# Hybrid decoder layer: conditioning parts 2 and 3 in whole, evenly spaced visits from a ring of four tiles of their own; part 4 from the shared ring in the output stage

## The chip, the cores and the metric

One core of a Trainium2 chip runs the kernel. The metric is device time in microseconds (us) of one execution. Three runs of the kernel before give a median of 1353.53 us, lowest 1352.69, highest 1353.59.

## The reference, cut to what matters

One layer of a hybrid decoder on 288 columns of tokens (256 of a prompt and 8 short sequences of 4), width 2048. Cut to what the kernel's stages and the change need:

```python
mod = silu(c) @ w_ada + b_ada                  # 9 conditions, 6 parts of 2048: "ada"
sh1, sc1, g1, sh2, sc2, g2 = split(mod, 6)     # parts 0, 1, 2, 3, 4, 5
h = rmsnorm(x, norm1) * (1 + sc1) + sh1
u_pool, z, xbc, dt = split(h @ w_in)           # one projection
pool_out = pool_mixer(u_pool)                  # trailing windows 2, 4, 8, 16, a linear map per group
ssd_out = rmsnorm(ssd(conv(xbc), dt) * silu(z))# 24 heads, 4 groups
x = x + g1 * (concat(pool_out, ssd_out) @ w_out)
h2 = rmsnorm(x, norm2) * (1 + sc2) + sh2
x = x + g2 * conv_ffn(h2)                      # gate, val and down projections
```

Part 2 (`g1`) is wanted first where the output projection is added to `x`; parts 3 and 4 (`sh2`, `sc2`) first where `h2` is made, ahead of the feed-forward stage.

## The kernel before, in words

**Stages.** The stages follow one another on the tensor engine (PE): the `xbc` projection in blocks of output tiles, then `mm_uz_*` (z and pooling columns), then the output projection `mm_out_0` to `mm_out_15`, then up/gate/val and down. Each projection multiplies a 128x128 weight block with 128x288 operands in three passes (lines 303, 304, 305: `whi*h`, `whi*l`, `wlo*h`), in a rounded 32-bit format. ACT casts each raw tile of weights to `whi` (L289) and DVE makes the rest `wlo` (L291).

**Work between.** While PE runs these projections, generators of other work are pulled a step at a time, and a scheduler orders each engine's instructions by priority and program order. `back` is the scan: its PE work (`cse`, `y`, `xt`, `bt`, `cb`, `s`, `yo`) is in plain 32-bit, a matmul of it being issued as several records. `late` is the pooling mixer: DVE makes `pout`, PE multiplies it (`pool`, L888). `adas` is the conditioning.

**Conditioning parts 2, 3, 4.** `ada_part_units` streams 32 tiles a part (`raw_adap`, 512 KB each: row block k, half h). `ada_mm` (L332) multiplies each tile twice into four 32-column strips of one accumulator `adap`, in plain 32-bit: a matmul is two records, so a tile is 4 records. A visit, the step between two yields, is `AY = 2` row blocks: 4 tiles, 8 matmuls, 16 records. When a part's eight visits are done, ACT copies the sum out (`asb_p`, L337), PE transposes it into an auxiliary accumulator (`adat_p`, L343), and DVE adds the bias in four instructions (`ada<-adat_p`, L420). The accumulator tiles called `aux` are shared by `adat_p`, `cse`, `y`, `pool` and others. Between `mm_dt` (the end of what both kernels have alike) and the feed-forward stage there are 24 visits.

**What sets their order.** `pull(adas, RA1 / AY)` in the last `xbc` block, `pull(adas, RA2 / AY)` in the uz stage and a pull after each `mm_out_m` add credit; at 1 a step is taken. The eight matmuls of a visit have no tie to one another: the scheduler may put other ready work between them.

**Tiles and queue.** All raw tiles, those of the projections and of the conditioning, come from one ring: 16 slots (`RAW0` 8 in pool `w0` and `RAW1` 8 in pool `w1`) up to the last `xbc` block, where `w0` is dropped, then 8, and 9 from `mm_out_5`. Every load is issued by SP, in program order, and a load waits on SP until its slot's last reader is done.

Of the kernel before, what the change touches and what calls it, by code (L numbers as in the profile page):

```python
# [25 lines left out]
NC9 = 1 + NB  # L26
# [10 lines left out]
ET = XT + len(UEARLY) + 3 * ZEARLY  # L37
EPS = 1e-6
WU = (14, 2, 2, 2, 6)
RAW0, RAW1, RAW2 = 8, 8, 1  # L40
SPLIT0, SPLIT1, SPLIT2 = 1, 2, 2
YK = 2
AQ = (4, 4, 4, 4, 4, 4)
# [5 lines left out]
TP = 0.4  # L49
TV, TL = 2.0, 2.8  # L50
GB = 4
AY = 2

RA1, RA2, RB1, RB2, RB3 = 0.5, 0.4, 1.0, 1.0, 1.0
TA, ADA_OUT = 4, 4
TK = 4
GA = (2, 3)
XM = (0, 2, 5, 9)
# [106 lines left out]
def kernel(ctx: ExitStack, tc, ins, outs):  # L165
# [98 lines left out]

    wp = [None]

    def load(key):
        off, cols = S.items[key]
        t = wp[0].tile([P, RAWC], F32, tag="raw", name="raw_" + "_".join(map(str, key)))
        nc.sync.dma_start(t[:, :cols], wflat[off:off + P * cols].rearrange("(p n) -> p n", p=P))  # L270
        return t

# [3 lines left out]

    def top_up():

        while queue and nloads[0] - min((n for n, _ in ahead.values()), default=nloads[0]) < RAW0 + RAW1:
            key = queue.popleft()  # L280
            ahead[key] = (nloads[0], load(key))
            nloads[0] += 1
# [69 lines left out]
    def ada_group_units(gi):  # L352
# [49 lines left out]
            nc.vector.tensor_tensor(o, src, b.unsqueeze(3).to_broadcast([P, 2, nj // 2, NC9]), ALU.add)  # L402
        ada_scale(0, 1, early[:, V_N1:V_N1 + KT], k0, gk)

    def ada_part_units(part, ay=1):
        ps = pa.tile([P, 512], F32, tag="ada", name=f"adap{part}")
        for k in range(KT):
            raws = [load(("adap", part, k, h)) for h in range(2)]
            for h in range(2):
                ada_mm(ps, raws[h], k, 0, 512, range(2 * h, 2 * h + 2))  # L410
            if k % ay == ay - 1:
                yield
        asb = ada_sb(ps, 512, f"p{part}")
        yield
        pt = ada_tr(asb, 512, f"p{part}")
        for i in range(4):
            o = ada[:, part].rearrange("p (j i) c -> p j i c", j=4)[:, :, i, :]
            b = bada[:, part].rearrange("p (j i) -> p j i", j=4)[:, :, i]
            src = pt[:, i * P:(i + 1) * P].rearrange("p (j c) -> p j c", j=4)[:, :, 0:NC9]
            nc.vector.tensor_tensor(o, src, b.unsqueeze(2).to_broadcast([P, 4, NC9]), ALU.add)  # L420
        if part == 4:
            ada_scale(1, 4, vec[:, V_N2:V_N2 + KT], 0, KT)
        yield

    def samp(ap):
        return ap.rearrange("p (b l) -> p b l", b=NB)
# [30 lines left out]
    class _W:  # L457


        def __init__(self):  # L460
            self.slots = {"raw": [], "whi": [], "wlo": []}
            self.i = {"raw": 0, "whi": 0, "wlo": 0}

        def add(self, pool, nraw, nsp):
            for tag, n in (("raw", nraw), ("whi", nsp), ("wlo", nsp)):
                m = len(self.slots[tag])
                if m:
                    r = self.i[tag] % m
                    self.slots[tag] = self.slots[tag][r:] + self.slots[tag][:r]
                    self.i[tag] = 0  # L470
                self.slots[tag] += [(pool, n)] * n

        def drop(self, pool):
            for tag, sl in self.slots.items():
                r = self.i[tag] % len(sl)
                self.slots[tag] = [x for x in sl[r:] + sl[:r] if x[0] is not pool]
                self.i[tag] = 0

        def tile(self, shape, dt, tag, name):
            pool, n = self.slots[tag][self.i[tag] % len(self.slots[tag])]  # L480
            self.i[tag] += 1
            return pool.tile(shape, dt, tag=tag, name=name, bufs=n)

    wp[0] = _W()
    wp[0].add(ctx.enter_context(tc.tile_pool(name="w1", bufs=1, side="right")), RAW1, SPLIT1)
    mx_ctx = ExitStack()
    mx = mx_ctx.enter_context(tc.tile_pool(name="mx", bufs=1))
    xa = []
# [10 lines left out]
    w0_ctx = ExitStack()  # L499
    w0 = w0_ctx.enter_context(tc.tile_pool(name="w0", bufs=1))  # L500
    shift(w0, 32)
    wp[0].add(w0, RAW0, SPLIT0)
    sx = [None]

    cvp = [mx.tile([P, 5, CW], F32, tag="cvp", name=f"cvp{g}", bufs=4) for g in range(4)]
# [159 lines left out]
    def drain(gen):  # L665
        for _ in gen:
            pass
# [236 lines left out]
    def chain(*gens):  # L904
        for gn in gens:
            yield from gn

    adas = chain(*(ada_part_units(p, AY) for p in (2, 3, 4)))
# [78 lines left out]
    def pull(gn, rate):  # L987

        credit[id(gn)] = credit.get(id(gn), 0.0) + rate
        while credit[id(gn)] >= 1:  # L990
            credit[id(gn)] -= 1
            next(gn, None)

    nloads[0] = len(first) + KT // 4
    for bi in range(len(BLOCKS)):
        last = bi + 1 == len(BLOCKS)
        top_up()
        if last:

            wp[0].drop(w0)  # L1000
            w0_ctx.close()
            sx[0] = mx_ctx.enter_context(tc.tile_pool(name="sx", bufs=1, reuse_waits="tile"))
            raw = load(("dt",))[:, :KT * NH].rearrange("p (k h) -> p k h", h=NH)
            wdt = wp[0].tile([P, RAWC], F32R, tag="whi", name="whi_dt")
            with tc.high_priority():
                nc.gpsimd.memset(wdt.bitcast(F32), 0.0)
                both = wdt[:, :DTW * KT].rearrange("p (k c) -> p k c", c=DTW)
                nc.scalar.copy(both[:, :, 0:NH], raw)
                nc.vector.tensor_tensor(both[:, :, 32:32 + NH], raw, both[:, :, 0:NH].bitcast(F32), ALU.subtract)
            ps = pm.tile([P, 512], F32, tag="mm", name="mm_dt")  # L1010
# [4 lines left out]
            late_states()  # L1015
            dt_stage(ps)
        elif bi == 4:
            nc.sync.dma_start(vec, ins["vec"])
        elif bi == 5:
            late_loads()  # L1020
        for i, m in enumerate(xbc_units(bi)):
            if not last:
                top_up()
                if bi == 0 and i in (3, 7, 13):
                    ci = {3: 2, 7: 3, 13: 4}[i]
                    ready["xbc", 0, ci] = split(fetch(("xbc", 0, ci)), 0, len(_xbc_chunks(0)[ci][1]) * P,
                                                f"xbc0_{ci}", pin=True)
                if i in VIS[bi]:
                    next(nxt)
                    top_up()  # L1030
            else:
                pull(back, 0.5 if m < 20 else RB1) if m >= 9 else None
                pull(adas, RA1 / AY)

    late = {}
    n = 0
# [1 line left out]
    for m in list(range(4 + 3 * ZEARLY, 16)) + ULATE:  # L1038
        for _ in uz_units(m):
            n += 1  # L1040
            for gn in late.values():
                pull(gn, 0.5)
            pull(adas, RA2 / AY)
            pull(back, RB2 if n <= zlast else RB3)
            if n == zlast:
                drain(back)
                back = ssd3
        if m < 4:
            late[m] = pool_units(m)
            next(late[m])  # L1050
    pull(adas, TA / AY)
    for h, (_, n) in enumerate(_halves(KT)):
        ready[("out", 0, h)] = split(load(("out", 0, h)), 0, n * P, f"out_0_{h}")
    drain(back)
# [33 lines left out]
    for i in range(KT // YK):  # L1088
        ps0 = next(out0)
        if i == 1:  # L1090
            for gn in late.values():
                drain(gn)
            for g in MIXK[NZ:]:
                mix_pool(g)
        if i == 3:
            psq = aux("ysum")
            col_sums(psq, ssq, ones[:, 0:1], True, True)
            _, rstdy = rstd_of(psq, NH * 64, "rstdy")
    mx_ctx.close()
    ff = ctx.enter_context(tc.tile_pool(name="ff", bufs=1, reuse_waits="tile"))  # L1100
    w2 = ctx.enter_context(tc.tile_pool(name="w2", bufs=1, reuse_waits="tile"))
# [49 lines left out]
    for m in range(16):  # L1151
        if m in XM:
            sl = slice(4 * XM.index(m), 4 * XM.index(m) + 4)
            nc.sync.dma_start(x[:, sl, :], ins["x"][:, sl, :])
        if m == 5:
            wp[0].add(w2, RAW2, SPLIT2)
        if m == 0:
            out_norm(ps0[0], m)
        else:
            for i, (pz, pp) in enumerate(out_units(m)):  # L1160
                if m == KT - 1 and i == 5:
                    all_but_last("ssum2")
# [295 lines left out]
```

## Time and profile before

| what | value |
|---|---|
| time, median of 3 runs | 1353.53 us |
| profiled execution: its time, its span | 1353.11 us, 1351.3 us |
| instructions | 26246 |
| PE busy | 1337.3 us (99%), 10517 matmul records |
| weight loads (PEld) | 1247.5 us (92%) |
| DVE, ACT, POOL busy | 820.0 us (61%), 579.4 us (43%), 227.5 us (17%) |
| moved by DMA | 323.19 MB |
| granted clock | 0.998 |

Times inside the trace are from the start of the span. In a line of the timeline the columns are start, length (from the first start of the run of alike instructions to the last end), engine, line, operation, output and inputs, shapes and count, and in brackets the idle time before it and what ended it. Matmuls overlap: a 128x288 pass is shown as 290 ns long, and the next starts 130 ns later. Idle of PE is the gap that its records leave; it is 14.0 us in the whole span (1351.3 less 1337.3).

### The profile page before, as it was taken

The page shows a single profiled execution, that of the slowest core. Times are in us where ns is not written, and L with a number is a line of the kernel's source. Part 1 is how long each engine was busy: PE and PEld are TensorE (multiplying, and loading weights), DVE is VectorE, ACT ScalarE, POOL GpSimd, SP SyncE. Part 2 cuts the span into 40 slices and gives each one's busy share as a digit, 9 for nine tenths or more (in the row PEclk, how much of TensorE's full clock was granted, in tenths as well). Part 3 has the DMA queues.
Part 4 walks back from the last instruction along what each step waited for, and adds up shares of the span by engine and source line. Part 5 has one row for each costly group of instructions (what it writes and reads, how often), then busy time and mean ns, then how long its engine had stood idle before and what let it go on. Part 6 is the DMA issues. An engine that isn't in the chain of part 4 may idle for free.

```text
span 1351.3 us, 26246 instructions
## 1 busy us (share of the span) xinstructions
PE 1337.3 (99%) x10517; PEld 1247.5 (92%) x10517; DVE 820.0 (61%) x1394; ACT 579.4 (43%) x911; POOL 227.5 (17%) x449
## 2 busy tenths in 40 slices
PE   9999999999999999999999999999999999999997
PEld 8889997776789889999999999999999999999997
DVE  5776568778665568645665445656655556566543
ACT  5343244587733335434443333434433343444442
POOL 0000012122122223111211001321120011132221
PEclk9999999999999999999999999999999999999999
DMA  9999768978888877787555555655555565566531
GB/s 373 405 408 368 252 242 324 340 257 295 324 332 323 320 253 257 249 280 265 181 187 182 162 178 183 204 183 196 181 180 164 184 191 184 187 207 194 179 119 70
DMA packets 97482, 323.19 MB, mean 239 GB/s; under 512 B 10768, under 2 KB 19920, under 8 KB 97360
## 3 DMA queue, kind: packets, MB, share of 16 engines
q1 hardware_dynamic: 93600, 310.79, 66.3%
q0 software_dynamic: 3184, 9.69, 2.0%
q8 instruction: 82, 1.34, 0.4%
q10 hardware_dynamic: 576, 1.03, 0.2%
q14 instruction: 40, 0.33, 0.1%
HBM read 309.78 MB, written 10.39 MB: 237 GB/s over the span
## 4 chain that ended last, share of the span: by engine, by line
PE 74%; DVE 1%; issue 0%; ACT 0%; DVEq 0%
PE mm_down L304 7%; PE mm_down L303 7%; PE mm_down L305 7%; PE mm_gate L303 6%; PE mm_val L304 6%; PE mm_gate L304 6%; PE mm_val L305 6%; PE mm_gate L305 6%; PE mm_val L303 6%; PE adap L332 3%; PE mm_out L303 2%; PE mm_out L304 2%; PE mm_out L305 2%; PE mm_up L303 1%; PE mm_up L304 1%; PE mm_up L305 1%
## 5 line engine op out<-in xcount | busy, mean ns | idle before, releaser
L304 PE MATMUL mm_down<-al,whi_down 128*128 128x288 f32 x688 | 202.5, 294 | 0.0
L303 PE MATMUL mm_down<-ah,whi_down 128*128 128x288 f32 x688 | 202.4, 294 | 0.0
L305 PE MATMUL mm_down<-ah,wlo_down 128*128 128x288 f32 x688 | 202.0, 294 | 0.0
L304 PE MATMUL mm_val<-h2l,whi_val 128*128 128x288 f32 x640 | 189.1, 296 | 0.0
L304 PE MATMUL mm_gate<-h2l,whi_gate 128*128 128x288 f32 x640 | 189.1, 295 | 0.0
L303 PE MATMUL mm_gate<-h2h,whi_gate 128*128 128x288 f32 x640 | 188.8, 295 | 0.0
L305 PE MATMUL mm_val<-h2h,wlo_val 128*128 128x288 f32 x640 | 188.4, 294 | 0.0
L305 PE MATMUL mm_gate<-h2h,wlo_gate 128*128 128x288 f32 x640 | 188.4, 294 | 0.0
L303 PE MATMUL mm_val<-h2h,whi_val 128*128 128x288 f32 x640 | 187.9, 294 | 0.0
L291 DVE TENSOR_TENSOR wlo_gate<-raw_gate,whi_gate 128x1024 fp32r<-128x1024 f32 x80 | 98.4, 1230 | 136.4 <-ACT whi_gate L289 136.3
L291 DVE TENSOR_TENSOR wlo_down<-raw_down,whi_down 128x1024 fp32r<-128x1024 f32 x96 | 107.5, 1120 | 116.9 <-ACT whi_down L289 114.4
L289 ACT CAST whi_down<-raw_down 128x1024 fp32r<-128x1024 f32 x96 | 92.3, 961 | 167.0 <-PE mm_down L304 118.0
L289 ACT CAST whi_gate<-raw_gate 128x1024 fp32r<-128x1024 f32 x80 | 83.8, 1049 | 160.0 <-PE mm_gate L304 64.9
L289 ACT CAST whi_val<-raw_val 128x1024 fp32r<-128x1024 f32 x80 | 84.1, 1051 | 119.5 <-issue 101.9
L303 PE MATMUL xbc<-h1h,whi_xbc 128*128 128x288 f32 x448 | 133.5, 301 | 0.8 <-ACT h1h L453 0.7
L304 PE MATMUL xbc<-h1l,whi_xbc 128*128 128x288 f32 x448 | 132.0, 296 | 0.0
L305 PE MATMUL xbc<-h1h,wlo_xbc 128*128 128x288 f32 x448 | 130.0, 295 | 0.0
L303 PEld LDWEIGHTS mm_down<-ah,whi_down 128*128 128x128 f32 x688 | 129.2, 188 | 0.0
L304 PEld LDWEIGHTS mm_down<-al,whi_down 128*128 128x128 f32 x688 | 129.1, 188 | 0.0
L305 PEld LDWEIGHTS mm_down<-ah,wlo_down 128*128 128x128 f32 x688 | 129.0, 187 | 0.0
L303 PEld LDWEIGHTS mm_gate<-h2h,whi_gate 128*128 128x128 f32 x640 | 120.3, 188 | 5.0 <-ACT ah L1221 3.4
L305 PEld LDWEIGHTS mm_gate<-h2h,wlo_gate 128*128 128x128 f32 x640 | 120.5, 188 | 0.0
(331 smaller groups left out, 2994.8 us busy)
## 6 DMA issues: line engine op xcount, KB each, us to landing
raw_adap<-wflat SPq DMA_DIRECT2D x128, 512.0 KB, 5.6
raw_gate<-wflat SPq DMA_DIRECT2D x80, 512.0 KB, 3.6
raw_val<-wflat SPq DMA_DIRECT2D x80, 512.0 KB, 3.9
raw_ada<-wflat SPq DMA_DIRECT2D x64, 512.0 KB, 9.6
raw_xbc<-wflat SPq DMA_DIRECT2D x50, 512.0 KB, 9.5
raw_down<-wflat SPq DMA_DIRECT2D x48, 512.0 KB, 3.6
raw_out<-wflat SPq DMA_DIRECT2D x32, 512.0 KB, 7.6
raw_down<-wflat SPq DMA_DIRECT2D x32, 384.0 KB, 3.1
```

Of the source, the lines that this page charges most:

```text
L289: yield nc.scalar.copy(hi[:, :n], raw[:, a:a + n])
L291: yield hi, lo, nc.vector.tensor_tensor(lo[:, :n], raw[:, a:a + n], hi[:, :n].bitcast(F32), ALU.subtract)
L303: nc.tensor.matmul(ps, whi[:, w], bh, start=first, stop=False)
L304: nc.tensor.matmul(ps, whi[:, w], bl, start=False, stop=False)
L305: nc.tensor.matmul(ps, wlo[:, w], bh, start=False, stop=last)
L332: nc.tensor.matmul(ps[32 * j:32 * j + 32, :nb], sc_c[:, k, :], raw[:, c:c + nb], start=(k == 0), stop=(k == KT - 1), tile_position=(0, 32 ...
```

## The change

- **Rings.** `RAW1` of 8 becomes 4, and a ring `rawa` of 4 (`RAWA`) stands beside it in the same pool. Up to the last `xbc` block the 12 and the 4 are one ring of 16, as before. At the last block `rawa` becomes a ring of its own; the shared ring has the other 4 and one more slot in pool `sx`, 5 in all. After parts 2 and 3 the four are put back into the shared ring. In the output stage pool `w2` brings 4 raw slots at `mm_out_2` (it was 1 at `mm_out_5`), and its split slots come at the same place.
- **Visits.** Parts 2 and 3 are done by a new generator, `ada_visits`. Its four loads are made two pulls ahead of the visit. The visit takes the last loaded tile first; its 2nd to 8th matmul are of high priority and all eight keep their program order. Pulls come at equal distances: `VA` sets 5 visits to the last `xbc` block and 11 to the uz stage and `mm_out_0`. A step is taken ahead of `dt_stage` as well.
- **End of a part.** Its transposes and its bias move to the next visit (`ada_end`), and the bias is one DVE instruction of high priority in place of four. Part 5 in the feed-forward stage has that instruction too.
- **Part 4** runs wholly in the output stage, from the shared ring, by the old generator. Its eight visits stand ahead of `mm_out_2`, 4, 6, 8, 10, 11, 12 and 13; before, one is ahead of `mm_out_0`, one within it, and six behind it.

The loads, the matmuls and their shapes are the same in number: 10517 PE records in both.

```diff
-RAW0, RAW1, RAW2 = 8, 8, 1
+RAW0, RAW1, RAWA, RAW2 = 8, 4, 4, 4
...
-AY = 2
-
-RA1, RA2, RB1, RB2, RB3 = 0.5, 0.4, 1.0, 1.0, 1.0
-TA, ADA_OUT = 4, 4
+VA = (5.01 / 28, 11.01 / 62)
+AK, AY, ADA_OUT = 2, 2, 4
+
+RB1, RB2, RB3 = 1.0, 1.0, 1.0
...
+    def ada_visits(parts, step):
+
+        plan = [(part, k0) for part in parts for k0 in range(0, KT, step)]
+        ahead, end = [], None
+
+        def chunks(v):
+            part, k0 = plan[v]
+            for k in range(k0, k0 + step):
+                for h in range(2):
+                    ahead.append((k, h, load(("adap", part, k, h), "rawa")))
+            yield
+            yield
+
+        yield from chunks(0)
+        for v, (part, k0) in enumerate(plan):
+            if end:
+                ada_end(*end)
+                end = None
+            if k0 == 0:
+                ps = pa.tile([P, 512], F32, tag="ada", name=f"adap{part}")
+            n = 0
+            for k, h, raw in ahead[::-1]:
+                for j in (2 * h, 2 * h + 1):
+                    with tc.high_priority() if n else nullcontext():
+                        i = nc.tensor.matmul(ps[32 * j:32 * j + 32, :], sc_c[:, k, :],
+                                             raw[:, 512 * (j % 2):512 * (j % 2) + 512], start=k == step - 1,
+                                             stop=k == KT - step, tile_position=(0, 32 * j))
+                    tc.keep_in_program_order(i)
+                    n += 1
+            ahead.clear()
+            if k0 + step == KT:
+                end = part, ada_sb(ps, 512, f"p{part}")
+            yield
+            yield
+            if v + 1 < len(plan):
+                yield from chunks(v + 1)
+        ada_end(*end)
+        yield
...
+    def ada_end(part, asb):
         pt = ada_tr(asb, 512, f"p{part}")
-        for i in range(4):
-            o = ada[:, part].rearrange("p (j i) c -> p j i c", j=4)[:, :, i, :]
-            b = bada[:, part].rearrange("p (j i) -> p j i", j=4)[:, :, i]
-            src = pt[:, i * P:(i + 1) * P].rearrange("p (j c) -> p j c", j=4)[:, :, 0:NC9]
-            nc.vector.tensor_tensor(o, src, b.unsqueeze(2).to_broadcast([P, 4, NC9]), ALU.add)
+        with tc.high_priority():
+            nc.vector.tensor_tensor(ada[:, part].rearrange("p (j i) c -> p i j c", j=4),
+                                    pt.rearrange("p (i j c) -> p i j c", i=4, j=4)[:, :, :, 0:NC9],
+                                    bada[:, part].rearrange("p (j i) -> p i j", j=4).unsqueeze(3)
+                                    .to_broadcast([P, 4, 4, NC9]), ALU.add)
...
+            wp[0].move("rawa", "raw", "rawa")
             w0_ctx.close()
             sx[0] = mx_ctx.enter_context(tc.tile_pool(name="sx", bufs=1, reuse_waits="tile"))
+            wp[0].add(sx[0], "raw", "raw", 1)
...
-                pull(adas, RA1 / AY)
+                pull(adas, 4 * VA[0])
...
-            pull(adas, RA2 / AY)
+            pull(adas, 4 * VA[1])
...
-    pull(adas, TA / AY)
+    drain(adas)
+    wp[0].move("rawa", "rawa", "raw")
+    adas = ada_part_units(4, AY)
...
-        if m == 5:
-            wp[0].add(w2, RAW2, SPLIT2)
+        if m == 2:
+            for tag, n in (("raw", RAW2), ("whi", SPLIT2), ("wlo", SPLIT2)):
+                wp[0].add(w2, tag, tag, n)
```

Line 332 of the kernel before is lines 332 (part 4) and 429 (parts 2 and 3) of the changed one; lines below move by some 54 to 60. In the rows that follow `raw_adap_14_0` is the tile of row block 14, half 0, `32x512` a matmul of the conditioning, `128x288` a pass of a projection; `x2` says that two such rows follow one another.

**PE, the eighth visit of part 3 near the end of the uz stage, before.** `y_2` is the scan's output of the last group.

```order
2020 L305 MATMUL mm_uz_4292<-h1h_130,wlo_uz_1_4422 128x288
2021 L332 MATMUL adap_3638<-raw_adap_14_0_4442,sc_c 32x512
2022 L821 MATMUL y_2_4397<-e_2_4359,xdt_4059 64x32 x2
2023 L824 MATMUL y_2_4397<-e_2_4359,xdt_4059 64x128 x2
2024 L827 MATMUL y_2_4397<-e_2_4359,xdt_4059 64x128
2025 L828 MATMUL y_2_4397<-ec_2_4360,s_3_4162 64x128
2026 L827 MATMUL y_2_4397<-e_2_4359,xdt_4059 64x128
2027 L828 MATMUL y_2_4397<-ec_2_4360,s_3_4162 64x128
2028 L332 MATMUL adap_3638<-raw_adap_14_0_4442,sc_c 32x512
2029 L332 MATMUL adap_3638<-raw_adap_14_1_4444,sc_c 32x512 x2
2030 L332 MATMUL adap_3638<-raw_adap_15_0_4450,sc_c 32x512 x2
2031 L332 MATMUL adap_3638<-raw_adap_15_1_4452,sc_c 32x512 x2
```

The changed kernel has that visit within `mm_out_0`:

```order
2092 L305 MATMUL mm_out_4625<-mixh_4578,wlo_out_0_4557 128x288
2093 L429 MATMUL adap_3643<-raw_adap_15_1_4474,sc_c 32x512 x2
2094 L429 MATMUL adap_3643<-raw_adap_15_0_4472,sc_c 32x512 x2
2095 L429 MATMUL adap_3643<-raw_adap_14_1_4470,sc_c 32x512 x2
2096 L429 MATMUL adap_3643<-raw_adap_14_0_4468,sc_c 32x512 x2
2097 L303 MATMUL mm_out_4625<-mixh_4579,whi_out_0_4555 128x288
```

Before, the visit is cut after its first matmul by the eight matmuls of `y_2`. In the changed kernel it is whole, with the last tile first. Seven of the 24 visits are cut before (one of them twice, the next place), none in the changed kernel.

**PE, the end of the last `xbc` block (the dt stage), before.** `dttr` and `cumt` are small transposes and sums for the time steps.

```order
1276 L305 MATMUL xbc_11_2690<-h1h_132,wlo_xbc_5_2664 128x288
1277 L332 MATMUL adap_2518<-raw_adap_4_0_2705,sc_c 32x512
1278 L582 MATMUL dttr<-early,dtt 128x24 x3
1279 L332 MATMUL adap_2518<-raw_adap_4_0_2705,sc_c 32x512
1280 L332 MATMUL adap_2518<-raw_adap_4_1_2707,sc_c 32x512 x2
1281 L332 MATMUL adap_2518<-raw_adap_5_0_2713,sc_c 32x512
1282 L594 MATMUL cumt<-tok,vec 128x48
1283 L596 MATMUL cumt<-tok,vec 128x24
1284 L597 MATMUL cumt<-tok,ones 128x48
1285 L599 MATMUL cumt<-tok,vec 128x24
1286 L332 MATMUL adap_2518<-raw_adap_5_0_2713,sc_c 32x512
1287 L332 MATMUL adap_2518<-raw_adap_5_1_2715,sc_c 32x512 x2
```

The same visit in the changed kernel, where `cumt` stands eleven rows ahead of it among passes of `xbc_13`:

```order
1305 L674 MATMUL totb<-dm,ones 128x192
1306 L680 MATMUL cumr<-vec,tok 128x128 x2
1307 L681 MATMUL cumr<-vec,tok 128x32
1308 L305 MATMUL xbc_13_2738<-h1h_132,wlo_xbc_6_2717 128x288
1309 L429 MATMUL adap_2511<-raw_adap_5_1_2711,sc_c 32x512 x2
1310 L429 MATMUL adap_2511<-raw_adap_5_0_2709,sc_c 32x512 x2
1311 L429 MATMUL adap_2511<-raw_adap_4_1_2707,sc_c 32x512 x2
1312 L429 MATMUL adap_2511<-raw_adap_4_0_2705,sc_c 32x512 x2
1313 L303 MATMUL xbc_14_2767<-h1h_129,whi_xbc_7_2763 128x288
```

Three pieces of one visit, with `dttr` and `cumt` between, become one piece, and `dttr` and `cumt` stand alone among passes of the projection.

**SP, the loads in the later uz stage, before.** All take the next slot of one ring of 8.

```order
208 L270 DMA raw_uz_0_4150<-wflat 128x1024
209 L270 DMA raw_uz_1_4238<-wflat 128x1024
210 L270 DMA raw_adap_10_0_4250<-wflat 128x1024
211 L270 DMA raw_adap_10_1_4252<-wflat 128x1024
212 L270 DMA raw_adap_11_0_4258<-wflat 128x1024
213 L270 DMA raw_adap_11_1_4260<-wflat 128x1024
214 L270 DMA raw_uz_0_4293<-wflat 128x1024
215 L270 DMA raw_adap_12_0_4343<-wflat 128x1024
```

The same stretch in the changed kernel; `raw_adap` takes the ring of 4, the others the ring of 5:

```order
208 L270 DMA raw_uz_0_4456<-wflat 128x1024
209 L270 DMA raw_uz_1_4511<-wflat 128x1024
210 L270 DMA raw_adap_8_0_4124<-wflat 128x1024
211 L270 DMA raw_adap_8_1_4126<-wflat 128x1024
212 L270 DMA raw_adap_9_0_4128<-wflat 128x1024
213 L270 DMA raw_adap_9_1_4130<-wflat 128x1024
214 L270 DMA raw_out_0_4553<-wflat 128x1024
215 L270 DMA raw_adap_10_0_4247<-wflat 128x1024
```

The four loads of a visit stay together in both. In the changed kernel the projections' tiles stand ahead of an earlier visit's (`raw_uz_0_4456`, the last uz tile pair, ahead of row blocks 8 and 9; before it stands behind row block 15), and `raw_adap_8_0` takes the slot that `raw_adap_6_0` had, which is the last that its visit reads.

More of the change, by code (lines that the diff above doesn't have):

```diff
@@ L265, with load @@
     wp = [None]
-    def load(key):
+    def load(key, ring="raw"):
         off, cols = S.items[key]
-        t = wp[0].tile([P, RAWC], F32, tag="raw", name="raw_" + "_".join(map(str, key)))
+        t = wp[0].tile([P, RAWC], F32, tag=ring, name="raw_" + "_".join(map(str, key)))
         nc.sync.dma_start(t[:, :cols], wflat[off:off + P * cols].rearrange("(p n) -> p n", p=P))
@@ L277, in top_up @@
     def top_up():
-        while queue and nloads[0] - min((n for n, _ in ahead.values()), default=nloads[0]) < RAW0 + RAW1:
+        while queue and nloads[0] - min((n for n, _ in ahead.values()), default=nloads[0]) < RAW0 + RAW1 + RAWA:
             key = queue.popleft()
@@ L414, in ada_part_units @@
         yield
+        ada_end(part, asb)
+        yield
+    def ada_end(part, asb):
         pt = ada_tr(asb, 512, f"p{part}")
-        for i in range(4):
-            o = ada[:, part].rearrange("p (j i) c -> p j i c", j=4)[:, :, i, :]
-            b = bada[:, part].rearrange("p (j i) -> p j i", j=4)[:, :, i]
-            src = pt[:, i * P:(i + 1) * P].rearrange("p (j c) -> p j c", j=4)[:, :, 0:NC9]
-            nc.vector.tensor_tensor(o, src, b.unsqueeze(2).to_broadcast([P, 4, NC9]), ALU.add)
+        with tc.high_priority():
[3 more added lines that the diff above has]
+                                    .to_broadcast([P, 4, 4, NC9]), ALU.add)
         if part == 4:
             ada_scale(1, 4, vec[:, V_N2:V_N2 + KT], 0, KT)
-        yield
     def samp(ap):
@@ L460, in __init__, with turn, add, move @@
         def __init__(self):
[L461 to L471, printed above, removed]
+            self.slots = {"raw": [], "rawa": [], "whi": [], "wlo": []}
+            self.i = dict.fromkeys(self.slots, 0)
+        def turn(self, ring):
+            sl = self.slots[ring]
+            r = self.i[ring] % len(sl) if sl else 0
+            self.slots[ring], self.i[ring] = sl[r:] + sl[:r], 0
+        def add(self, pool, ring, tag, n):
+            self.turn(ring)
+            self.slots[ring] += [(pool, tag, n)] * n
+        def move(self, tag, a, b):
+            self.turn(a)
+            self.turn(b)
+            self.slots[b] += [x for x in self.slots[a] if x[1] == tag]
+            self.slots[a] = [x for x in self.slots[a] if x[1] != tag]
         def drop(self, pool):
[L474 to L477, printed above, removed]
+            for ring in self.slots:
+                self.turn(ring)
+                self.slots[ring] = [x for x in self.slots[ring] if x[0] is not pool]
         def tile(self, shape, dt, tag, name):
-            pool, n = self.slots[tag][self.i[tag] % len(self.slots[tag])]
-            self.i[tag] += 1
+            pool, tag, n = self.slots[tag][self.ix(tag)]
             return pool.tile(shape, dt, tag=tag, name=name, bufs=n)
+        def ix(self, ring):
+            self.i[ring] += 1
+            return (self.i[ring] - 1) % len(self.slots[ring])
     wp[0] = _W()
-    wp[0].add(ctx.enter_context(tc.tile_pool(name="w1", bufs=1, side="right")), RAW1, SPLIT1)
+    w1 = ctx.enter_context(tc.tile_pool(name="w1", bufs=1, side="right"))
+    for ring, tag, n in (("raw", "raw", RAW1), ("raw", "rawa", RAWA), ("whi", "whi", SPLIT1), ("wlo", "wlo", SPLIT1)):
+        wp[0].add(w1, ring, tag, n)
     mx_ctx = ExitStack()
@@ L501 @@
     shift(w0, 32)
-    wp[0].add(w0, RAW0, SPLIT0)
+    for tag, n in (("raw", RAW0), ("whi", SPLIT0), ("wlo", SPLIT0)):
+        wp[0].add(w0, tag, tag, n)
     sx = [None]
@@ L906, in chain @@
             yield from gn
-    adas = chain(*(ada_part_units(p, AY) for p in (2, 3, 4)))
+    adas = ada_visits((2, 3), AK)
     with in_order(*(e.engine for e in (nc.tensor, nc.scalar, nc.vector))):
@@ L1015 @@
             late_states()
+            next(adas)
             dt_stage(ps)
@@ L1098 @@
             _, rstdy = rstd_of(psq, NH * 64, "rstdy")
+    wp[0].drop(sx[0])
     mx_ctx.close()
```

## The prediction

> **What bounds the kernel now.** The page comes first: engines and chain.
>
> ```profile
> span 1351.3 us, 26246 instructions
> ...
> PE 1337.3 (99%) x10517; PEld 1247.5 (92%) x10517; DVE 820.0 (61%) x1394; ACT 579.4 (43%) x911; POOL 227.5 (17%) x449
> ...
> PE 74%; DVE 1%; issue 0%; ACT 0%; DVEq 0%
> ```
>
> PE is busy for 1337.3 us, 99% of the span, and the chain that ended last is PE's own work. A change that leaves its 10517 records alone can only move what PE spends between them: the 14.0 us of idle (1351.3 less 1337.3), and time that hides inside "busy", since matmuls overlap and a drained pipeline still shows as busy. The waits of PE by name come next:
>
> ```profile
> PE cse L801 <- DVE ada L420: 1.0, 1, 1.0
> PE pool L888 <- DVE pout L883: 0.8, 1, 0.8
> ...
> PE dttr L582 <- DVE dtt L570: 0.6, 1, 0.6
> PE cb L751 <- DVE xde L740: 0.3, 1, 0.3
> ```
>
> These four, 2.7 us, are all in the stretch that the change reorders; most of PE's other idle is at the two ends of the span. The hidden part is read in the timeline. A whole visit in the output stage:
>
> ```profile
> 412.35 0.29 PE L305 MATMUL mm_outp<-mixh,wlo_out 128*128 128x288 f32 x1
> 412.58 1.92 PE L332 MATMUL adap<-raw_adap,sc_c 128*32 128x512 f32 x16
> 414.43 0.40 PE L303 MATMUL mm_out<-mixh,whi_out 128*128 128x288 f32 x1
> 414.67 0.30 PE L304 MATMUL mm_out<-mixl,whi_out 128*128 128x288 f32 x1
> 414.80 0.30 PE L305 MATMUL mm_out<-mixh,wlo_out 128*128 128x288 f32 x1
> ```
>
> From the last projection pass ahead to the second one behind, 2.32 us. The steady pitch of passes is 0.13 (414.67 to 414.80), so two passes are 0.27 and the visit costs 2.05. On either side the start is some 0.10 late against the pitch: a separate stretch of 32-bit work pays 0.2 for its two switches. Now a visit that the scan cuts, with the same scan step alone below it:
>
> ```profile
> 288.98 0.29 PE L305 MATMUL mm_uz<-h1h,wlo_uz 128*128 128x288 f32 x1
> 289.20 1.90 PE L332 MATMUL adap<-raw_adap,sc_c 128*32 128x512 f32 x10
> 291.04 0.31 PE L821 MATMUL y<-e,xdt 128*64 128x32 f32 x4
> ...
> 292.01 1.06 PE L332 MATMUL adap<-raw_adap,sc_c 128*32 128x512 f32 x6
> ...
> 293.23 0.29 PE L304 MATMUL mm_uz<-h1l,whi_uz 128*128 128x288 f32 x1
> ...
> 326.53 0.29 PE L303 MATMUL mm_uz<-h1h,whi_uz 128*128 128x288 f32 x1
> ...
> 327.96 0.29 PE L305 MATMUL mm_uz<-h1h,wlo_uz 128*128 128x288 f32 x1
> ```
>
> The cut one takes 293.23 - 288.98 - 0.27 = 3.98 us. The scan step alone takes 327.96 - 326.53 - 0.27 = 1.16, and 1.16 + 2.05 = 3.21. One cut costs 0.77 us, though nothing is idle. The reason is visible too: 16 records take 1.92 us, 10 take 1.90, 6 take 1.06, so a piece pays for a full round of four strips whether it fills it or not.
>
> **Part by part.**
>
> *Whole visits.* In the order, seven visits before are cut into fifteen pieces, and none in the changed kernel. The dearest form is a two-record piece that stands alone:
>
> ```profile
> 324.70 0.29 PE L304 MATMUL mm_uz<-h1l,whi_uz 128*128 128x288 f32 x1
> 324.92 1.04 PE L332 MATMUL adap<-raw_adap,sc_c 128*32 128x512 f32 x2
> ...
> 326.13 0.29 PE L303 MATMUL mm_uz<-h1h,whi_uz 128*128 128x288 f32 x1
> ...
> 332.54 0.38 PE L305 MATMUL mm_uz<-h1h,wlo_uz 128*128 128x288 f32 x1
> 332.85 1.92 PE L332 MATMUL adap<-raw_adap,sc_c 128*32 128x512 f32 x14
> ...
> 334.93 0.29 PE L304 MATMUL mm_uz<-h1l,whi_uz 128*128 128x288 f32 x1
> ```
>
> (1.43 - 0.27) + (2.39 - 0.27) - 2.05 = 1.23 us. The other seven cuts are joined to other 32-bit work and are priced at 0.77: 7 x 0.77 + 1.23 = 6.6 us. Bounds: 0.5 a cut (a two-record piece, 1.04, less two sixteenths of 1.92 and less some overlap) to 1.0, so 5 to 8.
>
> *Fewer stretches.* By the order, the stretches of 32-bit work between `mm_dt` and the feed-forward stage fall from 73 to 67. One of the six is the separate piece just priced; five at 0.2 give 1.0 us (0 to 1.5).
>
> *Stalls.* `cse` waits 1.0 us because its auxiliary accumulator is still held by the bias of part 2, whose last of four DVE instructions stands late among DVE's casts. They cost little themselves:
>
> ```profile
> L420 DVE TENSOR_TENSOR ada<-adat_p,early 128x36 f32<-128x36 f32 x16 | 2.3, 188 | 0.0
> ```
>
> In the changed kernel one instruction of high priority does it, so the tile is released at once; it has the elements of four, 0.2 to 0.8 us on DVE, which is not the bound. `dttr` is put six passes (0.8 us) later and `pool_1` gets a whole visit, a scan step and 32 passes (7.4 us by the rows above) after the uz tile it needs, in place of some 5. All four waits are taken as gone, 2.7 us (0 to 2.7). Sum of what goes: 6.6 + 1.0 + 2.7 = 10.3.
>
> *The ring of four.* This is the new wait. A visit reads four tiles, and the ring holds four, so the next four loads wait on SP until the visit reads its last tile. What is queued behind them on SP are the uz and out tiles, loaded far ahead (the ring of 5 has them a visit earlier in the order). How long it takes is shown by a visit whose loads met idle DMA queues, the one at 412.58:
>
> ```profile
> 413.67 1.75 SPq L270 DMA_DIRECT2D raw_adap<-wflat  x4
> ...
> L270 SPq DMA_DIRECT2D raw_adap<-wflat x4: 328/382/383, 413.7 to 415.0; - x4
> ...
> DMA to landing us min/median/max: 3.5/4.8/6.0
> ```
>
> The first load is issued 1.1 us after the visit starts, as its first tile is done; the slot that the changed kernel needs first is done three tiles later, 3 x 0.46, at 2.5. The fourth load is issued 1.3 after the first and lands 6.0 later, 7.3 to 7.4 in all. So visits from this ring cannot follow one another in less than 9.9 us. By the order, PE's work between the starts of two visits (passes at 0.133, 32-bit stretches at the prices above) is 11.5, 14.2, 11.5, 13.4, 10.7, 10.2, 12.5 and 15 us in part 2 and on to part 3, then 9.7, 9.5, 10.5, 10.4, 8.9, 10.6, 9.2. Four are short of 9.9, by 0.2 + 0.4 + 1.0 + 0.7 = 2.3 us. I take 2.5, with 0.5 to 5 for 0.3 either way at each. [...]
>
> *ACT and DVE.* A faster PE asks more of them, and in this stretch they are close to full:
>
> ```profile
> 275.00:300.00 25.00, 24.03 (x189) 18.06 (x191) 20.12 (x38) 20.29 (x46) 5.97 (x9) 1.00 0.71 246
> 300.00:325.00 25.00, 25.00 (x213) 17.43 (x206) 21.31 (x44) 21.97 (x50) 7.45 (x12) 1.00 0.83 294
> 325.00:350.00 25.00, 24.65 (x189) 17.62 (x190) 15.69 (x34) 14.64 (x27) 5.04 (x8) 1.00 0.79 291
> ```
>
> (Columns: width, then busy us of PE, PEld, DVE, ACT, POOL, clock, DMA share, GB/s.) At 20 to 22 of 25 us a scan step that comes closer behind its predecessor can find `e`, `cse` or `pout` late. No row has the new order; the nearest are the present waits, 2.7 us in 170 us. I take 1.5, between 0 and 5.
>
> *Output stage and after.* Part 4 as a whole moves there: two more visits of 2.05, which the uz stage and `mm_out_0` lose. The last four stand 8.3 us apart with six loads each, 3.1 MB, 379 GB/s, which the queues have shown here:
>
> ```profile
> GB/s 373 405 408 368 252 242 324 340 257 295 324 332 323 320 253 257 249 280 265 181 187 182 162 178 183 204 183 196 181 180 164 184 191 184 187 207 194 179 119 70
> ```
>
> The tiles that are ahead in the ring (12 slots from `mm_out_2`, 9 before) cover it: cost nothing; with the cover gone, six loads at 1.28 us a load (a third of the step from 3.5 to 6.0, and the 0.44 between issues) are 7.7 us of the 8.3, so at most 1 us. From the up projection on, the order is the same and PE never waits, so what is won stays won.
>
> *Sum.* -10.3 + 2.5 + 1.5 = -6.3 us on the profiled 1353.1, which is 0.4 below the median. On the median: 1353.5 - 6.3 = 1347.2.
>
> **The rivals.**
>
> *ACT and DVE set the pace (no change).* If the scan's chain on ACT and DVE, not PE, decides between 250 and 375, PE wins its cuts back as waits, the stalls included: 10.3 won, 8 to 12 lost, 1351 to 1355. For it: the 20 to 22 us above. Against: a slice of the same stage has them at 15 and 16, and PE waits there for only 2.1 us.
>
> *The visits' loads set the pace (slower).* If the loads on the ring of four do not meet idle queues but stand behind uz and state loads, each visit lands later. In the stage the queues are busy 0.71 to 0.93, and the median of all such loads is 5.6 us for one, not 3.5:
>
> ```profile
> raw_adap<-wflat SPq DMA_DIRECT2D x128, 512.0 KB, 5.6
> ...
> 225.00:250.00 25.00, 25.00 (x196) 20.19 (x195) 23.86 (x51) 9.78 (x11) 6.97 (x12) 1.00 0.93 350
> ```
>
> With 2.1 us more (5.6 - 3.5) the least distance is 12.0, and the list above is short of it by 0.5, 0.5, 1.3 and 1.8 in part 2 and 2.3, 2.5, 1.5, 1.6, 3.1, 1.4, 2.8 in part 3: 19.3 us, less 10.3 won, plus 1.5: 10.5 us slower, 1364. It decides from half of it: at 11.2 the list is short by 11 or so, and the change is 2 us slower. Against it: the ring of 5 lets the other loads be issued earlier, and a tile of 512 KB every 1.28 us leaves 9.9 us room for 7.7 tiles where about 6.5 are needed. By the Trainium skill's main page, Trainium Kernel Development and Optimization, section Best Practices, transfers should be double-buffered to overlap with compute; a ring of one visit is single-buffered for its visits, and this rival is what that rule warns of.
>
> *Larger gain.* The waits of the ring do not appear, since a visit's first matmul waits while PE still works off its queue, and cuts cost 1.0: -8 - 1.5 - 2.7 = -12.2, 1341.3 on the median.
>
> **How the numbers follow.** About 0.2%, 2.7 us, can be told from no change. Forecast (gain of 3 to 10 us): 0.58. Larger gain: 0.08. ACT and DVE: 0.17, of which a little lies on either side of no change. Loads: 0.17, of which three quarters are slower by over 2.7 us and the rest within. Faster is 0.58 + 0.08 + 0.02 = 0.68; slower 0.13 + 0.03 = 0.16; same 0.16. The range runs from the larger gain's 1341.0 to 1356.0, which takes in ACT and DVE and leaves out the heavier loads.
>
> **What would show it.** In the profile after: every `adap` row x16 between `mm_dt` and the up projection; no wait of `cse` on the bias (L460); waits of `adap` on `raw_adap`, or PE gaps ahead of visits, of 1 us at most and 2.5 in sum, in part 3 and not part 2; the first `mm_up` pass 6 us earlier. The forecast is wrong if `adap` waits on its loads by 1 us at most visits, or if waits of `cse`, `y` or `pool` on ACT and DVE sum to more than 5.

## The result and the profile after

The changed kernel takes 1348.73 us (median of 7 runs, 1348.28 to 1349.38) against 1353.52 (7 runs, 1352.69 to 1354.24): ratio 0.9965, 95% interval 0.9954 to 0.9977, or 4.8 us less. The forecast was 6.3 us less, 1347.2, in a range of 1341.0 to 1356.0. Its page, in the lines that answer to those of before:

```profile
span 1347.1 us, 26219 instructions
...
PE 1330.4 (99%) x10517; PEld 1245.7 (92%) x10517; DVE 822.6 (61%) x1382; ACT 576.2 (43%) x909; POOL 224.0 (17%) x449
```

PE's records are as many as before, and its busy time is 6.9 us less: the time came out of "busy", as cuts would have it, while idle grew by 2.7 us (14.0 before, 16.7 now). The waits of PE by name between 180 and 515 us, after:

```profile
PE adap L429 <- DMA raw_adap<-wflat: 1.1, 1, 1.1
PE pool L942 <- DVE pout L937: 1.1, 2, 0.7
PE cb L805 <- DVE xde L794: 0.8, 2, 0.6
PE cse L855 <- DVE yo L841: 0.4, 1, 0.4
PE mm_up L304 <- DVE h2l L496: 0.4, 1, 0.4
PE mm_up L303 <- ACT h2h L495: 0.4, 1, 0.4
PE y L875 <- DVE e L863: 0.2, 1, 0.2
```

The wait on the bias (1.0) and that of `dttr` (0.6) are gone; those of `pool` and `cb` stayed and grew by 0.8; `adap`, `cse`, `y` and `mm_up` are new. Three landmarks in PE's timeline split the 4.2 us of span, first before, then after:

```profile
185.36 0.29 PE L1013 MATMUL mm_dt<-h1h,whi_dt 128*128 128x288 f32 x1
500.87 0.80 PE L303 MATMUL mm_up<-h2h,whi_upk 128*128 128x288 f32 x4
539.32 0.29 PE L303 MATMUL mm_gate<-h2h,whi_gate 128*128 128x288 f32 x1
```

```profile
185.80 0.29 PE L1069 MATMUL mm_dt<-h1h,whi_dt 128*128 128x288 f32 x1
495.94 1.06 PE L303 MATMUL mm_up<-h2h,whi_upk 128*128 128x288 f32 x6 [0.35 <-ACT h2h L495]
535.08 0.29 PE L303 MATMUL mm_gate<-h2h,whi_gate 128*128 128x288 f32 x1
```

From `mm_dt` to `mm_up` 315.51 became 310.14, 5.37 less. From `mm_up` to `mm_gate` 38.45 became 39.14, 0.69 more, in a stage that was to stay as it was. The head, whose PE order is the same in both, is 0.44 later in this execution; over the profiles of the runs below, of either kernel, `mm_dt` starts between 185.4 and 186.0, so this is taken as scatter and not as part of the change. Without its gaps, PE's time from `mm_dt` to `mm_up` is 312.8 us before and 306.1 after, for the same 1545 records of 128x288: 6.7 us less.

### The profile page after: what moved, and what is told of

Its sections match the earlier page's. It is cut to its first block, busy times and chain, and to the rows that moved or that the text cites. A ratio compares the mean times of both kernels' runs of the same rounds, so it can differ in the third digit from the quotient of the medians.

```text
span 1347.1 us, 26219 instructions
## 1 busy us (share of the span) xinstructions
PE 1330.4 (99%) x10517; PEld 1245.7 (92%) x10517; DVE 822.6 (61%) x1382; ACT 576.2 (43%) x909; POOL 224.0 (17%) x449
## 4 chain that ended last, share of the span: by engine, by line
PE 93%; DVE 2%; DMA 2%; ACT 1%; issue 1%; POOL 0%; SPq 0%; DVEq 0%; POOLq 0%; ACTq 0%
PE mm_down L304 7%; PE mm_down L303 7%; PE mm_down L305 7%; PE mm_gate L303 6%; PE mm_val L304 6%; PE mm_gate L304 6%; PE mm_gate L305 6%; PE mm_val L305 6%; PE mm_val L303 6%; PE xbc L303 5%; PE xbc L304 4%; PE xbc L305 4%; PE adag L378 2%; PE adap L332 2%; PE mm_out L303 2%; PE mm_out L304 2%
```

## The experiments

**1. Untie the visits.** The changed kernel without the tie:

```diff
-                    with tc.high_priority() if n else nullcontext():
+                    with nullcontext():
...
-                    tc.keep_in_program_order(i)
```

> The changed kernel, but the eight matmuls of a visit of parts 2 and 3 lose their high priority and their fixed order; rings, spacing, part 4 and the single bias instruction stay. In its order four visits are cut again, into six more pieces. Theory (whole visits make the gain): six cuts at 0.77 us give back 4.6 us, about 1353.3 us, and the stretches of 32-bit work between mm_dt and the up projection cost 4 to 5 us more than in the changed kernel. Rival (own ring, even spacing and the place of part 4 make it): within 1 us of the changed kernel's 1348.7.

Measured: 1351.67 us (11 runs), ratio to before 0.9989 (0.998 to 0.9998), 2.9 us more than the changed kernel. What a visit looks like without the tie:

```profile
288.79 1.06 PE L429 MATMUL adap<-raw_adap,sc_c 128*32 128x512 f32 x6
...
290.75 1.06 PE L429 MATMUL adap<-raw_adap,sc_c 128*32 128x512 f32 x8
291.74 0.40 PE L854 MATMUL cse<-csr,selr 128*128 128x288 f32 x1
292.07 1.05 PE L429 MATMUL adap<-raw_adap,sc_c 128*32 128x512 f32 x2
```

Pieces of 6, 8 and 2 records take 1.06, 1.06 and 1.05 us where sixteen together take 1.92. Without its gaps PE's time from `mm_dt` to `mm_up` is 311.2 us, 5.1 more than in the changed kernel, where the theory had 4 to 5: some 0.85 for each of the six cuts that its timeline shows. The total loses less, since the waits of `pool`, `cb` and `cse` (2.3 us above) do not occur in that order. The rival (rings and places make the gain) falls for most of it.

**2. The tie alone, on the kernel before.**

```diff
-            nc.tensor.matmul(ps[32 * j:32 * j + 32, :nb], sc_c[:, k, :], raw[:, c:c + nb],
-                             start=(k == 0), stop=(k == KT - 1), tile_position=(0, 32 * j))
+            with tc.high_priority() if tie and not (lead and j == js[0]) else nullcontext():
+                i = nc.tensor.matmul(...)
+            if tie:
+                tc.keep_in_program_order(i)
```

(`tie` for parts 2, 3 and 4; `lead` marks a visit's first tile.)

> The kernel before with the tie alone: matmuls 2 to 8 of a visit of parts 2, 3 and 4 get high priority and keep program order; one ring, old spacing, four bias instructions. By its order one visit, in the dt stage, stays cut (three cuts), six are whole. Theory: 5 to 6 cuts fewer at 0.77, one of them 1.23, some 4.5 us less, about 1349; the waits of cse and pool may stay. Rival (the rings and places matter): no change, 1353.5.

Measured: 1349.90 us (10 runs), ratio 0.9972 (0.9962 to 0.9981): 3.5 us of the 4.8 with the tie and nothing else. Without its gaps PE's time from `mm_dt` to `mm_up` is 307.9 us, 4.9 less than before, for five cuts fewer. The timeline of this run at the place of the cut visit of 297.74 before:

```profile
297.00 0.29 PE L305 MATMUL mm_uz<-h1h,wlo_uz 128*128 128x288 f32 x1
297.21 1.92 PE L333 MATMUL adap<-raw_adap,sc_c 128*32 128x512 f32 x16
299.07 0.31 PE L825 MATMUL y<-e,xdt 128*64 128x32 f32 x4
...
300.28 0.30 PE L304 MATMUL mm_uz<-h1l,whi_uz 128*128 128x288 f32 x1
```

A whole visit with a scan step behind it: 300.28 - 297.00 - 0.27 = 3.01 us, against 3.98 for the cut form. At this place a cut cost 0.97 against the two side by side; 0.77 was worked out against the two standing apart, which pay one more pair of switches.

**3. One raw slot in pool `w2`, as before.** For the 0.69 us between `mm_up` and `mm_gate` there is a place in DVE's timeline, after the change:

```profile
494.09 0.95 DVE L291 TENSOR_TENSOR wlo_upk<-raw_upk,whi_upk 128x768 fp32r<-128x768 f32 x1
494.96 0.73 DVE L486 TENSOR_SCALAR h_n<-h_n,amul,ada 128x256 f32<-128x256 f32 x2
495.61 0.95 DVE L291 TENSOR_TENSOR wlo_upk<-raw_upk,whi_upk 128x768 fp32r<-128x768 f32 x1
496.47 0.45 DVE L496 TENSOR_TENSOR h2l<-h_n,h2h 128x288 fp32r<-128x288 f32 x1
497.52 0.46 DVE L496 TENSOR_TENSOR h2l<-h_n,h2h 128x288 fp32r<-128x288 f32 x1 [0.60 <-ACT h2h L495]
```

Two rests of later weights (`wlo_upk`, the second pair) stand ahead of `h2l`, for which PE waits. Before, they stand behind it:

```profile
500.44 0.46 DVE L454 TENSOR_TENSOR h2l<-h_n,h2h 128x288 fp32r<-128x288 f32 x1 [0.27 <-ACT h2h L453]
501.09 0.46 DVE L454 TENSOR_TENSOR h2l<-h_n,h2h 128x288 fp32r<-128x288 f32 x1 [0.18 <-ACT h2h L453]
...
502.13 1.93 DVE L291 TENSOR_TENSOR wlo_upk<-raw_upk,whi_upk 128x768 fp32r<-128x768 f32 x2
```

With more raw slots these weights are loaded earlier: the loads of that pair are issued at 480.1 and 483.4 after the change, and at 490.1 and 490.5 with one slot.

```diff
-RAW0, RAW1, RAWA, RAW2 = 8, 4, 4, 4
+RAW0, RAW1, RAWA, RAW2 = 8, 4, 4, 1
```

> The changed kernel with one raw slot in pool w2 in place of four. Its order puts the second pair of up-projection splits (wlo_upk) behind the first two h2l again, as before the change. Theory (the four slots let these splits stand ahead of h2 on ACT and DVE, and PE waits for h2 some 1.3 us longer): about 1347.4, no wait of mm_up on h2h or h2l. Rival (the late 1.3 us come from part 4's late end): 1348.7 as the changed kernel.

Measured: 1347.90 us (5 runs, 1347.28 to 1348.35), ratio 0.9959 (0.9946 to 0.9973). Its landmarks:

```profile
185.85 0.29 PE L1069 MATMUL mm_dt<-h1h,whi_dt 128*128 128x288 f32 x1
495.62 0.80 PE L303 MATMUL mm_up<-h2h,whi_upk 128*128 128x288 f32 x4
534.11 0.29 PE L303 MATMUL mm_gate<-h2h,whi_gate 128*128 128x288 f32 x1
```

From `mm_up` to `mm_gate` 38.49, the 38.45 of before, and `mm_up` starts 309.77 behind `mm_dt`, 0.37 earlier: 1.0 us in the profile, 0.8 in the medians. The four slots cost that and brought nothing. This is the fastest kernel of the study.

**4. The single bias instruction alone, on the kernel before.** The instruction of `ada_end`, put into `ada_part_units`:

```diff
-        for i in range(4):
...
-            nc.vector.tensor_tensor(o, src, b.unsqueeze(2).to_broadcast([P, 4, NC9]), ALU.add)
+        with tc.high_priority():
+            nc.vector.tensor_tensor(ada[:, part]..., pt..., bada[:, part]..., ALU.add)
```

> The kernel before with the single bias instruction of high priority alone. Theory: the wait of cse on the bias (1.0 us) goes, and one cut moves; 1352 to 1353, and no cse wait on the bias. Rival (the bias makes much of the gain by freeing the auxiliary accumulator): under 1351.

Measured: 1354.60 us (11 runs), ratio 1.0009 (1.0001 to 1.0018): 1.2 us slower. PE's waits between 180 and 515 us:

```profile
PE pool L888 <- DVE pout L883: 0.8, 1, 0.8
PE mm_out L305 <- DVE wlo_out L291: 0.7, 1, 0.7
PE dttr L582 <- DVE dtt L570: 0.6, 1, 0.6
PE mm_out L303 <- ACT whi_out L289: 0.6, 1, 0.6
PE cb L751 <- DVE xde L740: 0.4, 1, 0.4
```

The wait of `cse` on the bias is gone, as expected, and two waits of `mm_out` on its weights, 1.3 us, came in. That the total would rise was not expected; part 4's visit in `mm_out_0`, still cut there, lands at another place in that order, and what of the rise is due to that was not tried.

**5. Tie and single bias, on the kernel before.** The two diffs of runs 2 and 4 together.

> The kernel before with two parts of the change: the tie of the eight matmuls (parts 2 to 4) and the single bias instruction of high priority. PE's order is that of the tie alone (1349.9 us, where cse still lost 2 us to the held accumulator). Theory (the bias holds the accumulator, and the tie alone leaves that wait): the cse wait goes, 1 to 2 us less, 1348 to 1349. Rival (the bias instruction alone was 1 us slower, since it moves weight casts of the output stage): 1350 to 1351, with waits of mm_out on whi_out or wlo_out.

Measured: 1349.28 us (6 runs), ratio 0.9968 (0.9956 to 0.998), just above the expected 1348 to 1349 and 0.6 us under the tie alone, with intervals that overlap. No wait of `cse` on the bias, none of `mm_out` on weights; `pool` still waits 1.7. So two small parts of the change, without any ring, reach 4.4 of its 4.8 us. The own ring, the even spacing and part 4's place, none of them run alone on the kernel before, add about 1.2 us together by the ratios of this run and run 3, again with intervals that overlap.

**6. No ring of its own.** One raw slot in `w2`; the visits take the shared ring (now 9 slots), and part 4's visits are tied as in run 2.

```diff
-            wp[0].move("rawa", "raw", "rawa")
...
-                    ahead.append((k, h, load(("adap", part, k, h), "rawa")))
+                    ahead.append((k, h, load(("adap", part, k, h))))
```

> The changed kernel with one raw slot in pool w2 (1347.9 us as that step alone), but without the ring of four: visits of parts 2 and 3 take the shared ring of 9, and part 4's visits are tied too, since one comes to stand in mm_out_0. All visits whole. Theory (whole visits make the gain, the own ring only costs the one wait of adap, 1.0): within 1 us of 1347.9, no wait of adap on raw_adap, a wait or two of the scan in its place. Rival (the own ring frees the uz tiles and is needed for the even spacing): over 1349.5, waits on uz tiles or adap.

Measured: 1377.39 us (4 runs, 1373.12 to 1379.39), ratio 1.0171 (1.0155 to 1.0188): 29 us slower than with the ring, the largest miss of the study. PE now waits for the projections' weights:

```profile
PE xbc L303 <- ACT whi_xbc L289: 6.4, 3, 4.0
PE mm_uz L303 <- ACT whi_uz L289: 4.3, 6, 1.3
PE mm_out L303 <- ACT whi_out L289: 2.8, 2, 2.6
```

and ACT, which casts them, waits for their loads (between 180 and 400 us):

```profile
ACT whi_xbc L289 <- DMA raw_xbc<-wflat: 10.6, 4, 6.8
...
ACT whi_uz L289 <- DMA raw_uz<-wflat: 7.8, 6, 2.8
```

On SP 23 loads of conditioning go ahead of the first `raw_uz`, which is issued at 251.1; in the changed kernel 16 do, and it is issued at 226.9. The loads themselves land no later (in the median `raw_uz` in 5.1 us, 7.6 in the changed kernel). So loads made two pulls ahead of their visit stand in front on SP and hold slots that the projection needs first. Not all of the loss is waiting: between `mm_dt` and `mm_up` PE idles 20.2 us, 16.6 more than in run 3, of the 25 by which the two profiles differ. Some 5 us more go at half clock (the last section); the rest was not settled.

**7. The shared ring without the lead.** As the last, but a visit's loads are made at the visit:

```diff
+            yield
+            yield
             for k in range(k0, k0 + step):
                 for h in range(2):
                     ahead.append((k, h, load(("adap", part, k, h))))
-            yield
-            yield
```

> The shared ring of 9 as in the run of 1377.4 us (tied visits, even steps, one raw slot in w2), but a visit's four loads are made at the visit and not two pulls ahead. Theory (there the loads of conditioning, made ahead, stand in front of the projections' on SP and hold their slots, so weights come late; the ring itself is not the point): the 28 us go, 1348 to 1350, waits on whi and wlo under 2 us in all. Rival (a shared ring cannot feed evenly spaced whole visits): over 1360, waits of xbc and mm_uz on whi as there.

Measured: 1351.97 us (12 runs, 1350.50 to 1355.97), ratio 0.999 (0.9982 to 0.9998). 25 of the 29 us go with the lead, which is therefore what the shared ring could not bear; 4 us stay, which leaves it above the expected 1348 to 1350, and the runs scatter over 5.5 us. In its profile (an execution of 1350.65) PE waits 2.1 us for weights, most of it here:

```profile
PE mm_out L303 <- ACT whi_out L289: 1.1, 2, 0.9
...
PE mm_out L305 <- DVE wlo_out L291: 0.6, 1, 0.6
```

Whether the rest is the ring, the order or part 4's tie, which runs 6 to 9 have and run 3 has not, was not settled.

**8. Six visits in the last `xbc` block, part 4 tied.** One raw slot in `w2`, and:

```diff
-VA = (5.01 / 28, 11.01 / 62)
+VA = (6.01 / 28, 10.01 / 62)
```

> The changed kernel with one raw slot in pool w2, six visits in place of five in the last xbc block (ten in the uz stage), and part 4's visits tied. PE's order has three stretches of 32-bit work fewer to pay switches for, some 1.5 us. The visits from the ring of four come at 8.3, 9.9, 12.4, 9.4, 10.8, 11.8, 12.0, 11.4, 10.8, 11.8, 8.8, 9.5, 13.5, 10.3, 8.8 us of PE work. Theory (a visit can start 1.1 us + its loads' 7.4 to 9 us after the last one): waits of adap at the 8.3 and the two 8.8, some 0.3 to 1 each, 1.5 to 2 in all, and a time of 1347 to 1348.5. Rival (the 9.9 us of the prediction hold): waits of 1.6, 0.5, 1.1, 0.4 and 1.1, 4.7 us, 1350. Rival (loads land in 7.4 whatever else is queued): no waits, 1346.3.

Measured: 1352.79 us (11 runs, 1349.92 to 1354.34), ratio 0.9987 (0.9979 to 0.9996), 4.9 us slower than run 3, which has five visits and part 4 untied.

```profile
PE adap L432 <- DMA raw_adap<-wflat: 5.6, 4, 1.8
PE mm_out L303 <- ACT whi_out L289: 1.2, 1, 1.2
PE mm_out L305 <- DVE wlo_out L291: 1.2, 1, 1.2
```

The three visits with 8.3 to 8.8 us of work between them came 10.2 to 10.3 us apart. A visit with 9.4 waited 1.6 us, because its loads took 10.0 us to land, and one with 9.5 did not wait. Of the three expectations the prediction's 9.9 us comes nearest: 4.7 us of waits expected, 5.6 measured. None had the 2.4 us of `mm_out`, and 1352.79 is above all three. My own correction of it (1.5 to 2 us of waits) was too mild.

**9. A ring of five.** Part 4 tied, and:

```diff
-RAW0, RAW1, RAWA, RAW2 = 8, 4, 4, 4
+RAW0, RAW1, RAWA, RAW2 = 8, 3, 5, 1
```

> The changed kernel with one raw slot in w2 (1347.9 us), but 5 slots for the visits' own ring and 3 (with the one in sx, 4) for the shared one; part 4's visits tied, since one comes to stand in mm_out_0. One of a visit's loads can go before the visit ahead of it has run, three after. PE's order has visits as close as 7.2 and 8.0 us in part 3. Theory (the cadence is release plus landing of what could not go before; three loads instead of four, 1.3 us less, 8.6): waits of adap of 0.3, 1.4 and 0.6, and no waits of mm_uz: 1347.5 to 1348.5. Rival (the shared ring of 4 is too small for uz and out tiles): waits of mm_uz or mm_out on whi or wlo, over 1350.

Measured: 1350.64 us (11 runs), ratio 0.9979 (0.997 to 0.9988), 2.7 us slower than run 3.

```profile
PE mm_out L303 <- ACT whi_out L289: 2.0, 2, 1.9
...
PE mm_out L305 <- DVE wlo_out L291: 0.7, 1, 0.7
```

`adap` waits 0.3 us in all, though visits stand as close as 8.6 us: a slot more shortens the least distance. `mm_out` waits 2.7 us for its weights, and the time is where the rival had it. That the shared ring of four is the cause is not shown: the same two rows stand in runs 7 and 8 (1.7 and 2.4 us), where the shared ring has nine slots and five, and run 3 has neither row. What runs 7 to 9 share and run 3 lacks is part 4's tie, which was not run alone.

## Why the prediction was right, point by point

- **Whole visits and fewer stretches, 7.6 us: 6.6.** 5.37 us between `mm_dt` and `mm_up`, with waits there up from 2.7 to 3.6 and 0.35 at `mm_up` itself, leave 5.37 + 0.9 + 0.35 = 6.6, and PE's time without its gaps says the same (6.7). The mechanism is shown from both sides, by runs 1 and 2 (5.1 us more without the tie, 4.9 less with it alone). How the 6.6 divides is not shown: at the one place that could be compared a cut cost 0.97 and not 0.77, but seven such and the dear one would make 8.0, more than there is.
- **Stalls, 2.7 us gone: 1.6.** The bias and `dttr` went. `pool` and `cb` did not: the rows name `pout` and `xde` on DVE as what ends their wait, so a greater distance on PE did not remove it.
- **The ring of four, 2.5 us: 1.1.** One visit waits, the one at 8.9 that was priced at 1.0. Of the three priced at 9.2 to 9.7, which did not wait, two came 10.1 and 10.3 apart: PE's work between them was more than the order gave. The sum of 9.9 came out near for a wrong reason. The rows of that visit and its loads, after:

```profile
346.99 1.92 PE L429 MATMUL adap<-raw_adap,sc_c 128*32 128x512 f32 x16 [1.10 <-DMA raw_adap<-wflat]
```

```profile
338.03 1.75 SPq L270 DMA_DIRECT2D raw_adap<-wflat  x4
...
L270 SPq DMA_DIRECT2D raw_adap<-wflat x4: 328/370/382, 338.0 to 339.4; - x4
DMA to landing us min/median/max: 3.4/5.3/7.5
```

  The visit ahead starts at 336.94. The next loads are issued from 338.03, 1.1 us later and not 2.5, when only its first two tiles are read; so the first load does not wait for the tile read last, as the part on the change has it. The last lands at 339.4 + 7.5 = 346.9, 8.9 us after the first issue and not 7.3. In those 9 us the queues moved 2.93 MB, 0.8 more than the four tiles; in the 7.5 us of the visit at 412.58 it was 0.3 more. 1.1 + 8.9 is 10.0. It is no fixed distance: in parts 2 and 3 four loads took 7.4 to 9.6 us, and the visit 9.7 behind its predecessor, whose loads took 7.8, did not wait.
- **ACT and DVE, 1.5 us: 1.4** (`pool` 0.3 and `cb` 0.5 more, `cse` 0.4, `y` 0.2 new). The rival in which they set the pace did not come about.
- **Output stage, nothing: nothing.** No wait of part 4's visits.
- **From the up projection on, "the order is the same": wrong.** That holds for PE and not for DVE and ACT. It cost 1.0 us (0.35 + 0.69), shown by run 3. This is the step that failed.
- **The sum, and luck in it.** In the profiled pair the gain is 4.2 us, 2.1 short of 6.3: 1.0 by the step that failed, 0.44 by the head, 0.6 by the terms between. Those 0.6 are small by luck: visits and stalls gave 2.1 less than forecast, and the new waits took 1.5 less. In the medians, 4.8 us, it is 1.5 short. Of the signs, every visit of parts 2 to 4 is x16, no `cse` waits on the bias, and `adap` waits in part 3 alone; `mm_up` starts 4.9 us earlier and not 6.
- **The rival of the loads** did not come about with five visits in the `xbc` block. With six, `adap` waits 5.6 us (run 8), under a third of the 19.3 that the rival had. Without the own ring, loads made ahead cost 29 us, by when they are issued and not by how long they take to land (runs 6 and 7). The Trainium skill, Trainium Kernel Development and Optimization, section Best Practices, asks to double-buffer, so that DMA overlaps with compute. A ring of one visit does not, and its wait was 1.1 us in all; with a slot more 0.3 was left. Whether that slot pays is not shown (run 9), and no run has a ring of two visits.

## What to carry to other kernels

Where PE is 99% busy, look for time inside "busy": price a block whole, in pieces and beside its neighbours from the timeline, because pieces of 2, 6 and 8 records here cost the same. A tie of a few instructions gave 3.5 of 4.8 us. Loads made ahead needed a ring of their own: from a shared one they cost 29 us, 25 of which went when they were made at their use. When a change adds buffers, read the order of every engine behind them, since weights that arrive earlier may be put ahead of work that PE waits for.

## What was not expected of the hardware

Beside DVE's rests of weights POOL's small instructions grew long. Of the second half of `h_n`, before and after:

```profile
500.35 0.24 POOL L450 TENSOR_TENSOR h_n<-h_n,ada 128x32 f32<-128x32 f32 x1
```

```profile
495.55 1.48 POOL L492 TENSOR_TENSOR h_n<-h_n,ada 128x32 f32<-128x32 f32 x1
```

The same 128x32 instruction took 0.24 and 1.48 us; in the second case DVE's `wlo_upk` of 495.61 and `h2l` of 496.47 lie beside it, and `h2h` waits for POOL. In run 3, with no `wlo_upk` there, it took 0.24 again. By the Trainium skill, SBUF — State Buffer, section "SBUF: two separate sides", a DVE instruction with two inputs in SBUF and a POOL instruction that reads SBUF take one shared pair of ports by an exclusive lock, and the one that starts second is blocked. The trace agrees in that POOL's instruction ends at 497.03, 0.1 us after those two of DVE; it is recorded as starting 0.06 us ahead of them, so which had the ports first is not shown.

In run 6 the granted clock fell to a half for 3.4 us at three places between `mm_dt` and `mm_up`, each within 0.9 us of the end of a wait of PE (4.0, 2.2 and 2.6 us). The first of them:

```profile
205.00:208.40 3.40, 3.00 (x12) 3.00 (x13) 3.02 (x4) 1.30 (x2) 0.00 (x0) 0.50 0.20 42
```

(The columns are width, busy us of PE, PEld, DVE, ACT and POOL, clock, DMA share, GB/s.) Passes follow 0.24 us apart there and not 0.13, so the three cost some 5 us, an estimate: half of their 10.2 us. No wait of the other runs between these two marks is longer than 1.9 us, and none of those runs shows such a stretch there: a wait of over 2 us cost here more than its length.
